# Sixteen instead of ten pairs of up-projection strips computed with seven block products for eight

## The chip, the core and the metric

The kernel runs on one core of a Trainium2 chip. The metric is the device time of one execution in microseconds (us), as the median of several runs. The engines are named as in the profile: PE is the tensor engine's matmuls, PEld its weight loads, DVE the vector engine, ACT the scalar engine, POOL and SP the two engines that here only issue DMAs.

## What is computed

A decoder trunk of two layers over 256 tokens with a width of 2048, in float32. The part that the change touches is the ConvFFN of each layer:

```python
def conv_ffn(h, w_up, conv_w, conv_b, w_down):
    u = causal_depthwise_conv(h @ w_up, conv_w, conv_b)
    gate, val = u[..., :D_FF], u[..., D_FF:]
    return (jax.nn.silu(gate) * val) @ w_down
```

`h` is 256 x 2048 and `w_up` is 2048 x 11264 (two halves of 5632 columns: gates and values). The convolution runs over three tokens, column by column. Attention, the other projections and the per-layer embedding stand before and behind it and stay as they are.

## The kernel before, in words

**Strips and blocks.** Every projection is cut into strips of 512 weight columns. A strip has 16 blocks of 128 weight rows. Loads bring four blocks at a time: `raw`, 128 x 4 x 512 numbers, 1 MB, from a pool of four buffers (`NRAW`). SP issues the loads in program order, and each waits until the buffer that it gets is read out. Two blocks make a tile (a word used below for this unit of work). ACT rounds a tile into `whi` (L305), DVE takes the rest, `wlo = raw - whi` (L306); both have four buffers (`NWSP`). This is called the split of a tile. PE then forms for each block and each of the two token halves three products (L342 to L344): `xl*whi`, `xh*wlo`, `xh*whi`, so that a tile takes 12 matmuls.

**Pairs and halves.** A gate strip `s` and the value strip `v = s + 11` that belongs to it follow each other; there are 11 such pairs in a layer. A layer does them in two parts: pairs 0 to 4, then the down projection of these, then pairs 5 to 10, then the rest of the down projection. Behind each up strip come the scaling out of PSUM (L540, ACT), the transposition through DRAM (L243 on DVE, L246 and L254 on POOL's queue), and, one strip later, the convolution (L905 on ACT, L908 to L914 on DVE), SiLU and product (L926, L927, L150, L151).

**Seven products for eight.** For a pair handled by the class `Seven`, the first four weight blocks of both strips and the first four blocks of `h` are taken as a 2 x 2 by 2 x 2 product of larger blocks, and multiplied with seven block products in place of eight, by a Winograd scheme. A block product is 6 matmuls (L455). The sums of tokens that it needs are made once for a layer (`block_sums`, L410 to L422). The weight sums are made on DVE in the raw buffers (`add`, L439), each of the seven weight operands is split like a tile (`parts`, L445 and L446), and DVE and ACT join the partial results in PSUM (L478, L485, L495 to L498). The four accumulators `c11`, `c21` (gates) and `c12`, `c22` (values) then go on through the other 12 blocks.

**Where the seven products stand.** `begin` hangs two loads (`load`) and the first four products into the value strip of the pair before: as hooks ahead of tiles 1, 3, 5 and 7 of its eight (`HEADS8`), the load ahead of tile 0. `go_on` hangs products five, six and seven into the pair's own gate strip, ahead of its tiles 0, 1 and 3 of six (`TAILS`). Since a pair begins inside the pair before it, and `after` is made only for every second pair, the pairs with seven products are 2 and 4 of the first part and 6, 8 and 10 of the second: ten in two layers. `HEADS6` is never used.

**What sets the order.** All is recorded by one program. A scheduler places instructions on each engine by priority; splits, adds and the joins in PSUM carry `tc.high_priority(offset=AHEAD)`, so they stand ahead of the convolution. Each engine works in its order, and a semaphore holds an instruction until what it reads is there and what it overwrites is free.

**Names used below.** G is the gate strip of a seven-product pair, V the value strip behind it. Counted from zero, G's tiles are G0 to G5 and V's V0 to V5, with the products between them. `c11` lies in the bank with the tag att, `c21` in one of five banks with the tag acc, `c12` and `c22` in the double bank `two`.

## Time and profile before

| | us |
|---|---|
| runs (3): lowest, median, highest | 2289.43, 2289.99, 2290.62 |
| profiled execution: its time | 2287.39 |
| profiled execution: its span in the trace | 2285.6 |
| PE busy | 2273.2 (99%) |
| DVE busy | 1620.8 (71%) |
| ACT busy | 1298.6 (57%) |

The span runs from the first to the last instruction; 1.8 us lie around it. The granted clock of the tensor engine is 0.999 over the span. In the groups of the profile, "busy" is the union of an engine's instructions, and a matmul's end is modelled, so that the spacing of starts tells more than the length of one. The seven products (L455) run between 446.0 and 2014.9 us.

### The profile page before, as it was taken

The page shows a single profiled execution, that of the slowest core. Times are in us where ns is not written, and L with a number is a line of the kernel's source. Part 1 is how long each engine was busy: PE and PEld are TensorE (multiplying, and loading weights), DVE is VectorE, ACT ScalarE, POOL GpSimd, SP SyncE. Part 2 cuts the span into 40 slices and gives each one's busy share as a digit, 9 for nine tenths or more (in the row PEclk, how much of TensorE's full clock was granted, in tenths as well). Part 3 has the DMA queues.
Part 4 walks back from the last instruction along what each step waited for, and adds up shares of the span by engine and source line. Part 5 has one row for each costly group of instructions (what it writes and reads, how often), then busy time and mean ns, then how long its engine had stood idle before and what let it go on. Part 6 is the DMA issues. An engine that isn't in the chain of part 4 may idle for free.

```text
span 2285.6 us, 27930 instructions
## 1 busy us (share of the span) xinstructions
PE 2273.2 (99%) x10137; PEld 1882.0 (82%) x10137; DVE 1620.8 (71%) x2335; ACT 1298.6 (57%) x1734; POOL 327.7 (14%) x575
## 2 busy tenths in 40 slices
PE   9999999999999999999999999999999999999998
PEld 7888888888888888888888888888888888888887
DVE  7666667788755888865667665768875588886565
ACT  6554555666634666644565554566663466664454
POOL 0311111111100111101111331211110011110100
PEclk9999999999999999999999999999999999999999
DMA  8777767676755767767676776768675577776763
GB/s 304 258 239 243 231 228 257 220 266 234 246 196 190 267 227 243 268 205 246 207 265 236 252 263 223 260 215 273 234 255 188 196 254 234 242 264 215 239 223 120
DMA packets 98346, 538.43 MB, mean 236 GB/s; under 512 B 16672, under 2 KB 17568, under 8 KB 46752
## 3 DMA queue, kind: packets, MB, share of 16 engines
q1 hardware_dynamic: 63360, 435.46, 54.6%
q0 software_dynamic: 32560, 95.98, 13.9%
q10 hardware_dynamic: 2288, 5.21, 0.6%
q8 instruction: 79, 1.29, 0.2%
q14 instruction: 59, 0.48, 0.1%
HBM read 486.52 MB, written 50.07 MB: 235 GB/s over the span
## 4 chain that ended last, share of the span: by engine, by line
PE 99%; DMA 0%; ACT 0%; DVE 0%; issue 0%; POOL 0%; SPq 0%; ACTq 0%
PE accv L343 26%; PE accv L342 26%; PE accv L344 26%; PE two L343 3%; PE two L342 3%; PE two L344 3%; PE gates L342 2%; PE gates L343 2%; PE gates L455 2%; PE gates L344 2%; PE two L455 2%; PE two L554 1%; PE keys L554 0%; DMA raw<-in_wqkv 0%; DMA turned<-there 0%; ACT whi L305 0%
## 5 line engine op out<-in xcount | busy, mean ns | idle before, releaser
L306 DVE TENSOR_TENSOR wlo<-raw,whi 128x1024 fp32r<-128x1024 f32 (+1 forms) x784 | 951.1, 1215 | 547.5 <-ACT whi L305 545.8
L305 ACT ACTIVATE whi<-raw 128x1024 fp32r<-128x1024 f32 (+1 forms) x784 | 825.7, 1054 | 776.1 <-PE accv L344 609.9
L342 PE MATMUL accv<-whi,h 128*128 128x512 f32 (+1 forms) x1688 | 655.3, 388 | 1.0 <-DVE h L144 0.9
L344 PE MATMUL accv<-whi,h 128*128 128x512 f32 (+1 forms) x1688 | 656.3, 389 | 0.0
L343 PE MATMUL accv<-wlo,h 128*128 128x512 f32 (+1 forms) x1688 | 655.9, 389 | 0.3 <-DVE wlo L306 0.2
L342 PEld LDWEIGHTS accv<-whi,h 128*128 128x128 f32 x1688 | 316.8, 188 | 67.4 <-ACT whi L305 1.6
L343 PEld LDWEIGHTS accv<-wlo,h 128*128 128x128 f32 x1688 | 316.9, 188 | 66.8 <-DVE wlo L306 2.0
L344 PEld LDWEIGHTS accv<-whi,h 128*128 128x128 f32 x1688 | 316.9, 188 | 64.9
L246 POOL DMA_DIRECT2D there<-y x162 | 91.4, 565 | 1275.4 <-DVE y L243 1257.1
L342 PE MATMUL accv<-whi,g 128*128 128x512 f32 x704 | 273.9, 389 | 0.0
L343 PE MATMUL accv<-wlo,g 128*128 128x512 f32 x704 | 273.9, 389 | 0.0
L344 PE MATMUL accv<-whi,g 128*128 128x512 f32 x704 | 273.9, 389 | 0.0
L254 POOL DMA_DIRECT2D turned<-there x324 | 189.6, 592 | 448.9 <-DMA there<-y 174.3
L343 PEld LDWEIGHTS accv<-wlo,g 128*128 128x128 f32 x704 | 132.1, 188 | 27.5
L342 PEld LDWEIGHTS accv<-whi,g 128*128 128x128 f32 x704 | 132.1, 188 | 27.4
L344 PEld LDWEIGHTS accv<-whi,g 128*128 128x128 f32 x704 | 132.1, 188 | 27.4
L446 DVE TENSOR_TENSOR wlo<-raw,whi 128x1024 fp32r<-128x1024 f32 x70 | 85.4, 1221 | 27.8 <-ACT whi L445 27.8
L445 ACT ACTIVATE whi<-raw 128x1024 fp32r<-128x1024 f32 x70 | 74.0, 1057 | 53.0 <-PE accv L344 47.6
L342 PE MATMUL gates<-whi,h 128*128 128x512 f32 x240 | 93.4, 389 | 0.0
L344 PE MATMUL gates<-whi,h 128*128 128x512 f32 x240 | 93.4, 389 | 0.0
L343 PE MATMUL gates<-wlo,h 128*128 128x512 f32 x240 | 93.4, 389 | 0.0
L342 PE MATMUL two<-whi,h 128*128 128x512 f32 x240 | 93.4, 389 | 0.0
(206 smaller groups left out, 2427.4 us busy)
## 6 DMA issues: line engine op xcount, KB each, us to landing
raw<-in_wup SPq DMA_DIRECT2D x176, 1024.0 KB, 5.5
raw<-in_wdn SPq DMA_DIRECT2D x88, 1024.0 KB, 5.0
there<-y POOLq DMA_DIRECT2D x171, 256.0 KB, 5.1
turned<-there POOLq DMA_DIRECT2D x324, 128.0 KB, 4.6
raw<-in_wqkv SPq DMA_DIRECT2D x40, 1024.0 KB, 5.7
raw<-in_wpg SPq DMA_DIRECT2D x32, 1024.0 KB, 4.8
raw<-in_wkv SPq DMA_DIRECT2D x24, 1024.0 KB, 5.6
raw<-in_wo_a SPq DMA_DIRECT2D x16, 1024.0 KB, 5.3
```

Source lines behind the costliest of these rows:

```text
L246: nc.gpsimd.dma_start(there[t * P : (t + 1) * P], y)
L254: nc.gpsimd.dma_start(z[32 * b : 32 * b + 32].rearrange("p a o r -> p a (o r)"), back[b])
L305: last["high"] = nc.scalar.activation(hi[:, c], r, AF.Copy).ins
L306: last["low weights"] = nc.vector.tensor_tensor(lo[:, c], r, f32(hi[:, c]), op=OP.subtract).ins
L342: nc.tensor.matmul(ps, xl, hi, start=first, stop=False, skip_group_check=again)
L343: nc.tensor.matmul(ps, xh, lo, start=False, stop=False, skip_group_check=again)
L344: nc.tensor.matmul(ps, xh, hi, start=False, stop=final, skip_group_check=again)
L445: last["high"] = nc.scalar.activation(hi, r, AF.Copy).ins
L446: last["low weights"] = nc.vector.tensor_tensor(lo, r, f32(hi), op=OP.subtract).ins
L455: nc.tensor.matmul(ps, x, y, start=begins, stop=ends, skip_group_check=True)
L554: run.append(nc.tensor.matmul(*args, skip_group_check=True, **kw).ins)
```

## The change

Every pair but the first two of the first part and the first of the second now gets seven: 2, 3 and 4, and 6 to 10, sixteen in two layers. Pairs then overlap: the four first products of the next pair stand in V of the one before, ahead of tiles 1, 2, 4 and 5 of its six (`HEADS[6]`), with the two loads ahead of tile 0. So that two pairs have room in PSUM, every second pair takes `c12` and `c22` from the five acc banks (`two=False`), and each accumulator is now allocated at the product that first writes it. `block_sums` makes the same sums with smaller operations and in other buffers (`room()`). `strip_among`, `go_on` and `end` are rewritten for this; `both` is defined and not called.

```diff
-HEADS8, HEADS6, TAILS = (1, 3, 5, 7), (1, 2, 4, 5), (0, 1, 3)
+HEADS, TAILS = {8: (1, 3, 5, 7), 6: (1, 2, 4, 5)}, (0, 1, 3)
...
-        f = four("whole").rearrange("p (k c) -> p k c", k=4)
-        for k in range(4):
-            nc.vector.tensor_tensor(f[:, k], f32(xs[k][:, :S]), f32(xs[k][:, S:]), op=OP.add)
...
+        out = [[] for _ in range(4)]
+        for i in range(2):
+            f, m = (room().rearrange("p (a c) -> p a c", c=P) for _ in range(2))
...
+        def value_bank(self, o):
+            if not self.two:
+                return bank("values", "acc")
+            if o == 0:
+                self.banks = two_banks()
+            return self.banks[:, o]
...
         def first(self):
-            self.c11, self.c21 = bank("gates"), bank("gates", "acc")
-            values = two_banks()
-            self.c12, self.c22 = values[:, 0], values[:, 1]
+            self.c11 = bank("gates")
...
         def second(self):
+            self.c12 = self.value_bank(0)
...
         def third(self):
+            self.c21 = bank("gates", "acc")
...
         def fourth(self):
+            self.c22 = self.value_bank(1)
...
         def begin(self, tiles):
-            do = [self.first, self.second, self.third, self.fourth]
-            self.hooks = {0: self.load, **dict(zip({8: HEADS8, 6: HEADS6}[tiles], do))}
-            return self.hooks
+            return {0: self.load, **dict(zip(HEADS[tiles], (self.first, self.second, self.third, self.fourth)))}
 
         def go_on(self):
-            return dict(zip(TAILS, (self.fifth, self.sixth, self.seventh)))
...
+            hooks = dict(zip(TAILS, (self.fifth, self.sixth, self.seventh)))
+            yield strip_among(self.W, self.strips[0], self.xs, hooks, [self.c11, self.c21], 4, self.base)
+
+        def end(self, hooks):
+            return strip_among(self.W, self.strips[1], self.xs, hooks, [self.c12, self.c22], 4, self.base)
...
+    def hooked(it, hooks):
+
+        for i in range(KB * 8):
+            if i in hooks:
+                hooks[i]()
+            try:
+                tile = next(it)
+            except StopIteration:
+                return
+            yield tile
...
                     v = s + FB // 4
-                    after = Seven(W, s + 1, v + 1, xs, sums) if j % 2 == (late is not None) and s + 1 in strips else None
+                    sums_next = (j > 0 or late is None) and s + 1 in strips
+                    after = Seven(W, s + 1, v + 1, xs, sums, two=j % 2 == 0) if sums_next else None
                     if j == 0 and late is not None:
                         yield from products([(W, s, 0), (W, v, 0)], xs, late, None)
-                        continue
-                    base = 4 if now else 0
-                    tiles = (len(xs) - base) // 2
-                    yield strip_among(W, s, xs, now.go_on() if now else {}, now and [now.c11, now.c21], base)
-                    yield strip_among(W, v, xs, after.begin(tiles) if after else {}, now and [now.c12, now.c22], base)
+                    elif now is None:
+                        yield strip_among(W, s, xs, {})
+                        yield strip_among(W, v, xs, after.begin(8) if after else {})
+                    else:
+                        yield from now.go_on()
+                        yield now.end(after.begin(6) if after else {})
                     now = after
```

On SP's queue, in the first layer's second part, this stood before from the last load of pair 6's gate strip on (`raw_1121`: tiles G4 and G5; the next three loads are the value strip's, the fifth is of the plain pair behind):

```order
L288 DMA raw_1121_6115<-in_wup 128x2048
L288 DMA raw_1139_6197<-in_wup 128x2048
L288 DMA raw_1144_6231<-in_wup 128x2048
L288 DMA raw_1149_6265<-in_wup 128x2048
L288 DMA raw_1165_6337<-in_wup 128x2048
```

And this stands there now (`raw_1131`: tiles G4 and G5; L471 are the two loads of `load` for pair 7; `raw_1151` holds V0 and V1, `raw_1163` V2 and V3):

```order
L288 DMA raw_1131_6139<-in_wup 128x2048
L471 DMA raw_1149_6221<-in_wup 128x2048
L471 DMA raw_1150_6223<-in_wup 128x2048
L288 DMA raw_1151_6225<-in_wup 128x2048
L288 DMA raw_1163_6287<-in_wup 128x2048
```

The first load of the value strip was second in this row and is now fourth. In the built program the fourth load of the row takes the buffer that the split of G3 frees, before and now; the second takes that of G1's split.

On DVE, before, from the split of G5 of the same pair on (`wlo_1141` is the split of V0, L243 the transposition of the gate strip's result, L908 the convolution):

```order
L306 TENSOR_TENSOR wlo_1125_6134<-raw_1121_6115,whi_1124_6133 128x1024
L914 TENSOR_TENSOR gate_1101_5992<-gate_1101_5992,over_1102_6005 128x7x4
L306 TENSOR_TENSOR wlo_1141_6200<-raw_1139_6197,whi_1140_6199 128x1024
L914 TENSOR_TENSOR gate_1101_5992<-gate_1101_5992,over_1103_6008 128x7x4x2
L306 TENSOR_TENSOR wlo_1143_6216<-raw_1139_6197,whi_1142_6215 128x1024
L306 TENSOR_TENSOR wlo_1146_6234<-raw_1144_6231,whi_1145_6233 128x1024
L243 STREAM_TRANSPOSE y_1129_6154<-u_1126_6149 128x4x4x32
L306 TENSOR_TENSOR wlo_1148_6250<-raw_1144_6231,whi_1147_6249 128x1024
```

And now, from the split of G5 on (`wlo_1153` is the split of V0, L456 are the splits for the products of pair 7 and L449 its weight sums):

```order
L306 TENSOR_TENSOR wlo_1135_6158<-raw_1131_6139,whi_1134_6157 128x1024
L934 TENSOR_TENSOR gate_1111_6016<-gate_1111_6016,over_1112_6029 128x7x4
L934 TENSOR_TENSOR gate_1111_6016<-gate_1111_6016,over_1113_6032 128x7x4x2
L306 TENSOR_TENSOR wlo_1153_6228<-raw_1151_6225,whi_1152_6227 128x1024
L456 TENSOR_TENSOR wlo_1157_6246<-raw_1149_6221,whi_1156_6245 128x1024
L449 TENSOR_TENSOR raw_1149_6221<-raw_1149_6221,raw_1150_6223 128x1024
L306 TENSOR_TENSOR wlo_1159_6259<-raw_1151_6225,whi_1158_6258 128x1024
L449 TENSOR_TENSOR raw_1150_6223<-raw_1150_6223 128x1024
L456 TENSOR_TENSOR wlo_1162_6276<-raw_1149_6221,whi_1161_6275 128x1024
L243 STREAM_TRANSPOSE y_1139_6178<-u_1136_6173 128x4x4x32
L449 TENSOR_TENSOR raw_1149_6221<-raw_1149_6221,raw_1150_6223 128x1024
L306 TENSOR_TENSOR wlo_1165_6290<-raw_1163_6287,whi_1164_6289 128x1024
```

Behind the split of V0, DVE's queue now holds two more splits and three weight sums up to the split of V2 (the last row), where before the split of V2 was the second behind it.

More of the change, by code (lines that the diff above doesn't have):

```diff
@@ L404, in block_sums @@
     def block_sums(xs):
-        f = four("whole").rearrange("p (k c) -> p k c", k=4)
-        for k in range(4):
-            nc.vector.tensor_tensor(f[:, k], f32(xs[k][:, :S]), f32(xs[k][:, S:]), op=OP.add)
-        (a11, a21), (a12, a22) = ((f[:, k : k + 2, :P], f[:, k : k + 2, P:]) for k in (0, 2))
-        m = four("sums").rearrange("p (q i c) -> p q i c", q=4, i=2)
-        nc.vector.tensor_tensor(m[:, 0], a21, a22, op=OP.subtract)
-        nc.vector.tensor_tensor(m[:, 1], a11, a21, op=OP.subtract)
@@ L415, in block_sums @@
-        nc.vector.tensor_tensor(m[:, 2], m[:, 0], a11, op=OP.subtract)
-        nc.vector.tensor_tensor(m[:, 3], m[:, 2], a12, op=OP.add)
-        out = []
-        for q in (0, 2):
+        out = [[] for _ in range(4)]
+        for i in range(2):
+            f, m = (room().rearrange("p (a c) -> p a c", c=P) for _ in range(2))
+            for a, k in enumerate((i, 2 + i)):
+                whole = f[:, 2 * a : 2 * a + 2].rearrange("p t c -> p (t c)")
+                nc.vector.tensor_tensor(whole, f32(xs[k][:, :S]), f32(xs[k][:, S:]), op=OP.add)
+            a11, a21, a12, a22 = (f[:, a] for a in range(4))
+            nc.vector.tensor_tensor(m[:, 0], a21, a22, op=OP.subtract)
+            nc.vector.tensor_tensor(m[:, 1], a11, a21, op=OP.subtract)
+            nc.vector.tensor_tensor(m[:, 2], m[:, 0], a11, op=OP.subtract)
+            nc.vector.tensor_tensor(m[:, 3], m[:, 2], a12, op=OP.add)
@@ L419, in block_sums @@
             hi, lo = (rt("sum", dt=F32R) for _ in range(2))
-            src = m[:, q : q + 2].rearrange("p q i c -> p (q i c)")
+            src = m.rearrange("p q c -> p (q c)")
             nc.scalar.activation(hi, src, AF.Copy)
             nc.vector.tensor_tensor(lo, src, f32(hi), op=OP.subtract)
-            for j in range(2):
-                out.append([[t[:, (2 * j + i) * P : (2 * j + i + 1) * P] for t in (hi, lo)] for i in range(2)])
+            for q in range(4):
+                out[q].append([t[:, q * P : (q + 1) * P] for t in (hi, lo)])
@@ L425, in block_sums, with __init__, token @@
         return out
     class Seven:
-        def __init__(self, W, s0, s1, xs, sums):
-            self.strips = W, s0, s1
-            self.sums = sums
-            self.token = lambda k, t: [[xs[k + i][:, c + t * P : c + (t + 1) * P] for c in (0, S)] for i in range(2)]
+        def __init__(self, W, s0, s1, xs, sums, base=0, two=True):
+            self.W, self.strips, self.base, self.two = W, (s0, s1), base, two
+            self.xs, self.sums = xs, sums
+        def token(self, k, t):
+            return [[self.xs[k + i][:, c + t * P : c + (t + 1) * P] for c in (0, S)] for i in range(2)]
@@ L457, in load @@
         def load(self):
-            W, s0, s1 = self.strips
             raws = []
-            for s in (s0, s1):
+            for s in self.strips:
                 raw = wraw.tile([P, RAW, 512], F32, tag="raw", name=nm("raw"))
-                nc.sync.dma_start(raw, W[s, 0])
+                nc.sync.dma_start(raw, self.W[s, self.base // RAW])
                 raws.append(raw)
@@ L509, in begin, with both, strip_among @@
         def begin(self, tiles):
[L510 to L512 removed]
+            return {0: self.load, **dict(zip(HEADS[tiles], (self.first, self.second, self.third, self.fourth)))}
         def go_on(self):
[L515 to L532 removed]
+            hooks = dict(zip(TAILS, (self.fifth, self.sixth, self.seventh)))
+            yield strip_among(self.W, self.strips[0], self.xs, hooks, [self.c11, self.c21], 4, self.base)
+        def end(self, hooks):
+            return strip_among(self.W, self.strips[1], self.xs, hooks, [self.c12, self.c22], 4, self.base)
+        def both(self):
+            yield from self.go_on()
+            yield self.end({})
+    def hooked(it, hooks):
[7 more added lines that the diff above has]
+            yield tile
+    def strip_among(W, s, xs, hooks, begun=None, skip=0, base=0):
+        n = len(xs) - skip
+        ps = begun or [bank("accv", "acc") for _ in range(2)]
+        it = hooked(weights(W, s, n, base=base + skip), hooks)
+        for k, o, hi, lo in (g for group in steps(it, n, 2) for g in group):
+            add_block(ps[o], xs[skip + k], o, hi, lo, k == 0 and not begun, k == n - 1, begun is not None)
         return ps
```

10 lines of the change are left out of this document (removed).

## Prediction

> **What bounds the kernel now.** First the page's head and the busy shares:
>
> ```profile
> span 2285.6 us, 27930 instructions
> ...
> PE 2273.2 (99%) x10137; PEld 1882.0 (82%) x10137; DVE 1620.8 (71%) x2335; ACT 1298.6 (57%) x1734; POOL 327.7 (14%) x575
> ```
>
> PE has work nearly all the time. Whether it also waits is in the view of the waits, for PE alone:
>
> ```profile
> PE warm L125 <- DVE zero L122: 1.2, 1, 1.2
> PE accv L342 <- DVE h L144: 0.9, 2, 0.7
> PE accv L343 <- DVE wlo L306: 0.2, 1, 0.2
> ```
>
> That is all: 2.3 us in the whole span. So time is saved by taking matmuls out, provided that nothing else becomes late. What a matmul costs is the spacing of starts. The timeline of PE gives it between the first product of a gate strip G and the first matmul of its value strip V, 90 matmuls later (12 for each of six tiles, 18 in products):
>
> ```profile
> 836.31 0.39 PE L455 MATMUL gates<-whi,h 128*128 128x512 f32 x1
> ...
> 856.71 0.39 PE L342 MATMUL two<-whi,h 128*128 128x512 f32 x1
> 856.94 0.39 PE L343 MATMUL two<-wlo,h 128*128 128x512 f32 x1
> ```
>
> 20.40 us by 90 is 0.2267 us each; the 0.39 us in the row overlap. Next, how full the other engines are, in windows of exactly one seven-product pair and one plain pair (7 x 6 + 24 x 6 and 32 x 6 matmuls, 378 in all, 85.68 us):
>
> ```profile
> 807.98:893.66 85.68, 85.68 (x379) 70.95 (x378) 72.49 (x110) 54.68 (x72) 13.89 (x24) 1.00 0.73 246
> 893.66:979.34 85.68, 85.68 (x379) 70.95 (x378) 71.29 (x110) 54.84 (x72) 13.89 (x24) 1.00 0.73 247
> ```
>
> In the order PE, PEld, DVE, ACT, POOL: DVE is busy for 72.5 and 71.3 us of 85.68, ACT for 55. The reader should keep DVE's 84% in mind, because the change turns the plain pair, where DVE rests, into another full one.
>
> **What is removed.** Six pairs lose one block product: 6 x 6 = 36 matmuls (the order of PE shows exactly 36 fewer). 36 x 0.2267 = 8.2 us. The bytes loaded stay the same, two loads of 1 MB standing for the first load of each strip.
>
> **What is added on DVE.** A seven-product pair has three splits more than a plain one, four weight sums and four joins in PSUM. Their spacing on DVE:
>
> ```profile
> 450.11 1.22 DVE L439 TENSOR_TENSOR raw<-raw,raw 128x1024 f32<-128x1024 f32 x1
> 451.25 2.35 DVE L306 TENSOR_TENSOR wlo<-raw,whi 128x1024 fp32r<-128x1024 f32 x2
> ...
> 836.40 0.69 DVE L496 TENSOR_TENSOR gates<-gates,part 128x512 f32<-128x512 f32 x1
> 837.00 0.70 DVE L243 STREAM_TRANSPOSE y<-u 128x512 f32<-128x512 f32 x1
> 837.63 0.67 DVE L497 TENSOR_TENSOR two<-part,gates 128x512 f32<-128x512 f32 x1
> ...
> 844.33 1.61 DVE L908 SCALAR_TENSOR_TENSOR gate<-turned,vec,gate 128x240 f32<-128x240 f32 x4
> ...
> 847.76 0.32 DVE L912 TENSOR_TENSOR over<-turned,vec 128x28 f32<-128x28 f32 x2
> ```
>
> A sum takes 1.14 us from start to start, a split 1.13 (2.35 less one length of 1.22), a join 0.60, a transposition 0.63, a convolution step 0.38 (1.61 less 0.46, by three); the four small ones of a strip (L912, L914) 0.12 each. So 7 x 1.14 + 4 x 0.60 = 10.4 us more than in a plain pair. Both together are 71.9 us (mean of the two windows), a seven-product pair is (71.9 + 10.4) / 2 = 41.1 us of DVE. Where pairs overlap PE needs 7 x 6 + 24 x 6 = 186 matmuls for one, 42.15 us. DVE has 1.0 us left in each: 98% full, but not over. That DVE can hold such a share is seen in the trace, in a stretch in which PE never stopped:
>
> ```profile
> 440.00:480.00 40.00, 40.00 (x179) 33.10 (x178) 38.05 (x52) 27.91 (x37) 4.60 (x8) 1.00 0.59 203
> ```
>
> ACT gets three roundings more and two copies, about 4 us; (54.8 + 4) / 2 is 29 us of 42.15: covered.
>
> A rule of the Trainium skill speaks against this (VectorE: DVE Perf Modes, section "The DRAIN you can't avoid"): the next vector operation does not start before the pipeline of the last is empty. By it each of some 60 operations of a pair would cost its full length, about 0.08 us more than the spacing above, and DVE would be the bound. The rows just shown contradict it: 837.00 is before 836.40 + 0.69. I keep it as a rival with a small chance.
>
> **What is moved: the load of the value strip.** While a pair's sums stay in two of the four raw buffers, the other loads share the rest. In the new order the loads that follow G's last one on SP are two for the next pair, and only then the first of V, which waits for the split of G3 and so is fourth in a burst. Before, the load in that place belonged to the last tiles of V and had time. Its row, three times, with the start of G ahead of it, and what SP's issue and landing were (last number of the DMA row: us to landing):
>
> ```profile
> 750.63 0.39 PE L455 MATMUL gates<-whi,h 128*128 128x512 f32 x1
> 758.76 0.33 SPq L288 DMA_DIRECT2D raw<-in_wup  x1
> raw<-in_wup SPq DMA_DIRECT2D x1, 1024.0 KB, 9.4
> 844.43 0.33 SPq L288 DMA_DIRECT2D raw<-in_wup  x1
> raw<-in_wup SPq DMA_DIRECT2D x1, 1024.0 KB, 11.6
> 2009.72 0.39 PE L455 MATMUL gates<-whi,h 128*128 128x512 f32 x1
> 2017.83 0.33 SPq L288 DMA_DIRECT2D raw<-in_wup  x1
> raw<-in_wup SPq DMA_DIRECT2D x1, 1024.0 KB, 12.3
> ```
>
> It is issued 8.1 us after G starts and lands at 17.5, 19.7 and 20.4 us. From landing to a split tile takes the rounding and the subtraction:
>
> ```profile
> 852.20 1.04 ACT L305 ACTIVATE whi<-raw 128x1024 fp32r<-128x1024 f32 x1
> 853.28 1.23 DVE L306 TENSOR_TENSOR wlo<-raw,whi 128x1024 fp32r<-128x1024 f32 x1 [2.08 <-ACT whi L305]
> ```
>
> 852.20 to 854.51, 2.3 us, 2.4 with the semaphore. PE reaches V at 20.4 us and reads `wlo` with its second matmul, at 20.6. So V0 is late by 17.5 + 2.4 - 20.6 (not late), by 1.5 and by 2.2 us, 1.2 in the mean. In the kernel before V0's load was second in the burst. The wait is ACT's, and queued behind it on ACT are the roundings for the next pair's first product and for V1 and the scaling of `c11`; on DVE all behind the split of V0 waits with it. This comes to pass in the first seven-product pair of each part, 4 times: 4.9 us. These places are well founded, since up to V0 nothing differs from the trace.
>
> **And the later pairs, where DVE has no rest before.** There are 8 more such places (3 in the first part, 7, 8 and 9 in the second, in two layers). Where V0 is late DVE has stood idle, and it then has the rest of V and of G in one queue. From the split of V0 to that of G3 of the next pair it has all of a pair but the part from G3 to V0: three splits, eight convolution steps, a transposition and four small ones, 3 x 1.14 + 8 x 0.38 + 0.63 + 0.5 = 7.6 us. That leaves 41.1 - 7.6 = 33.5 us. Then G3's buffer is free, V's load is issued, lands after L us, and 2.4 us later V0 is split: a loop of 35.9 + L against PE's 42.15. PE stalls from L = 6.25 us on. For L in such a place the trace has a load alone, and one that is third in a burst:
>
> ```profile
> raw<-in_wup SPq DMA_DIRECT2D x1, 1024.0 KB, 5.0
> raw<-in_wup SPq DMA_DIRECT2D x1, 1024.0 KB, 6.6
> ```
>
> (issued at 830.44 and 843.30). The ends are 5.0 (nothing lost) and 12.3 (6.1 us lost each). What drew the fourth load out is the traffic on POOL's queue at that time, as the windows in its flight and before it show (last two numbers: DMA share, GB/s), with POOL's four `turned` transfers:
>
> ```profile
> 850.00:857.00 7.00, 7.00 (x33) 5.79 (x32) 4.09 (x5) 3.79 (x5) 0.00 (x0) 1.00 1.03 229
> 842.00:844.00 2.00, 2.00 (x10) 1.67 (x9) 2.00 (x3) 1.02 (x2) 0.56 (x1) 1.00 1.00 416
> ...
> 846.06 2.34 POOL L254 DMA_DIRECT2D turned<-there x4 [3.45 <-ACT whi L305]
> ```
>
> The 16 engines are full in both, but carry half the bytes once `turned` is on them. In a later pair the gate strip's transpositions stand behind the splits of G2 and beside G3, so `turned` comes some 5 us behind the load, not 2, and I place L near the third in a burst: 7.1 us. The loop is 43.0, 0.85 us lost in each, 8 x 0.85 = 6.8 us.
>
> The page "DMA: Bandwidth & Descriptors" of the Trainium skill (section "Anatomy of one DMA") has 2.0 us and the bytes at 436 GB/s for a DMA; 1 MB would land in an estimated 4.4 us, V0 would never be late and the sum would be the 8.2 us alone. The lone load above took 5.0, and none in a burst was near 4.4.
>
> **Inside V.** Behind V0's split stand, up to V2's, seven operations of 1.14 us and a transposition, 8.6 us; PE is there after 36 matmuls, 8.2 us. 0.4 us late; the loop holds this already, except behind the last late V of each part: 4 x 0.4 = 1.6 us.
>
> **Edits at nothing.** `block_sums` has 14 operations on DVE for 10, some half as long, about 0.3 us a layer while the down projection ahead has DVE at rest. The bank of `c11` must be scaled out before the next pair's first product: `c11` ends six matmuls before G does, and V0 gives 2.7 us more; the scaling is one row of ACT:
>
> ```profile
> 855.55 0.69 ACT L540 ACTIVATE u<-gates,rcol 128x512 f32<-128x512 f32 x1 [0.25 <-PE gates L344]
> ```
>
> 1.4 + 2.7 - 0.7 leaves 3.4 us; with V0's load late, three roundings stand ahead of it on ACT, and about 1 us is left. If that goes too, PE waits for ACT at the first product. The acc banks come round after five uses, a strip and more.
>
> **Sum.** -8.2 + 4.9 + 6.8 + 1.6 = +5.1 us. The profiled execution took 2287.4 us (span 2285.6 and 1.8 around it) and would take 2292.5; the median of the runs is 2.6 us above it, so 2295.1 us. About 0.2%, 4.6 us, is what a measurement of this kernel can tell.
>
> **Rivals.**
>
> Nothing is late (faster). The lead of four split buffers and a quick load hide all, and the matmuls alone count: 2290.0 - 8.2 = 2281.8 us. For it: PE waits nowhere today, the stretch at 440 us with DVE at 95%, loads alone at 5.0 us. Against it: two of the three landings above. 0.20.
>
> Only the first places are late: L is under 6.25 in the later pairs, 4.9 + 1.6 us remain, 2288.3 us. For it: the new spacing of the loads on DVE's queue. Against it: DVE's 1.0 us of rest. 0.15.
>
> The load is drawn out everywhere (slower by more). If `turned` meets V's load in the later pairs as it does at 844 us, L is 9.4 or above, and the loop 45.3: 3.15 us x 8 = 25 us, with the 6.5 us of the first places 2290.0 + 23.5 = 2313.5 us. It decides from L = 9 on. For it: three rows. Against it: the later `turned`. 0.11.
>
> DVE is the bound: each operation costs its length, 60 x 0.08 us added to 41.1 gives 45.9 us a pair, 3.7 over PE in 12 overlapping strips, 45 us: 2326 us. Against it the rows above. 0.04. That is the rule on the drain.
>
> That the change doesn't do what it says is excluded by the order of PE.
>
> **How the numbers follow.** My forecast has 0.50 and its own range is 2290 to 2301: L from 6.6 to 7.6 and the first places from 0.5 to 1.9 us each. Of it 0.20 lies within 0.2%, 0.30 above. The rival of the first places gives 0.13 to no change and 0.02 to faster. So faster 0.20 + 0.02 = 0.22, same 0.20 + 0.13 = 0.33, slower 0.30 + 0.11 + 0.04 = 0.45. The range goes from just under the first rival, 2281, to 2304; what is left out is most of the two slow rivals and some tail, under 0.2.
>
> **What the new profile would show.** PE's waits, now 2.3 us, would name `whi` or `wlo` and add up to some 13 us; they would lie at the first tile of V, about 12 places, with ACT's rounding of it ended by the DMA `raw<-in_wup`. The issue of that load would be 8.1 us after G in the first pairs, later (about 11) in the following ones. DVE's busy time per overlapping pair would be near 41 us. I am wrong if PE's waits stay under 3 us (nothing is late), if they lie at other tiles or on PSUM banks (the wrong wait), or if the load lands within 6 us in a burst.

## The result, and the profile after

| | before | changed |
|---|---|---|
| runs, of one chip | 4 | 4 |
| lowest, median, highest | 2289.15, 2289.71, 2290.62 | 2304.74, 2310.62, 2313.31 |
| profiled execution, its span | 2287.39, 2285.6 | 2304.74, 2303.0 |
| ratio of the times | | 1.0087, 95% interval 1.0070 to 1.0103 |

The change makes the kernel slower by 0.9%, where 0.2% was forecast. The sign is as forecast, the size is outside the range (2281 to 2304). The profiled execution is the fastest of the four; what is read from it explains 17.4 us of span, and the median lies 6 us above it. The spread of the runs has grown from 1.5 to 8.6 us.

The head of the page and its busy shares:

```profile
span 2303.0 us, 27972 instructions
...
PE 2273.0 (99%) x10101; PEld 1875.6 (81%) x10101; DVE 1676.3 (73%) x2409; ACT 1312.1 (57%) x1764; POOL 327.7 (14%) x575
```

The 36 matmuls are gone (10101 for 10137), and DVE has 55 us more (six pairs by 10.4 us were forecast to be 62). PE's "99%" is the same only by rounding: outside its busy time lie 30.0 us of the span now and 12.4 us before. And PE is as busy as before with 8.2 us of matmuls fewer, since the modelled end of a matmul that waits covers a part of the wait. The view of PE's waits:

```profile
PE gates L342 <- DVE values L507: 9.2, 6, 1.8
PE gates L342 <- DVE two L507: 4.3, 6, 1.5
PE two L343 <- DVE wlo L306: 2.3, 6, 0.8
PE values L343 <- DVE wlo L306: 1.3, 2, 1.1
```

The last two lines are waits at the splits of V, but V0 itself, where the prediction placed them, is late in two pairs only (the first of each second part, by 0.9 and 1.7 us); the others stand at later tiles of V, mostly V2. The first two are new: 12 waits, one in the G behind each overlap, at the second token half of G0, the first matmul that goes on with `c21`, and they end with L507 on DVE. By the spacing of starts over 0.2267 us (the matmul after a wait is late by another 0.11) the waits in V cost some 7 us and those at `c21` 16.8 us.

Here is one of them, first PE (its row names the releaser), then DVE in the same 4 us:

```profile
885.04 0.39 PE L342 MATMUL gates<-whi,h 128*128 128x512 f32 x1
...
886.17 0.39 PE L344 MATMUL gates<-whi,h 128*128 128x512 f32 x1
888.02 0.50 PE L342 MATMUL gates<-whi,h 128*128 128x512 f32 x1 [1.46 <-DVE values L507]
```

```profile
884.24 0.69 DVE L505 TENSOR_TENSOR part<-values,part 128x512 f32<-128x512 f32 x1
884.94 1.22 DVE L456 TENSOR_TENSOR wlo<-raw,whi 128x1024 fp32r<-128x1024 f32 x1
886.08 0.69 DVE L506 TENSOR_TENSOR gates<-gates,part 128x512 f32<-128x512 f32 x1
886.68 0.69 DVE L508 TENSOR_TENSOR values<-values,part 128x512 f32<-128x512 f32 x1
887.28 0.69 DVE L507 TENSOR_TENSOR values<-part,gates 128x512 f32<-128x512 f32 x1
```

L506 has put the sum into `c21` at 886.77, and PE still waits until 887.97. The reason is in the operands: L507 is `c22 = q - c21`. It reads `c21`, so PE may not write it until L507 is done. In the kernel before, the same join ended at 838.30 (its row is in the prediction), and PE came to `c21` 12 matmuls after 836.31, at 839.03. The slack was 0.73 us, and it stood in rows that the prediction quotes.

The load that the prediction speaks of, in the pair before that wait, from the timeline: G, the load's issue, ACT's rounding that waited for it, the split of V0, and the same load's issue one pair later:

```profile
840.56 0.39 PE L465 MATMUL gates<-whi,h 128*128 128x512 f32 x1
...
850.81 0.33 SPq L288 DMA_DIRECT2D raw<-in_wup  x1
...
858.86 1.06 ACT L305 ACTIVATE whi<-raw 128x1024 fp32r<-128x1024 f32 x1 [5.20 <-DMA raw<-in_wup]
...
859.95 1.23 DVE L306 TENSOR_TENSOR wlo<-raw,whi 128x1024 fp32r<-128x1024 f32 x1 [2.63 <-ACT whi L305]
...
894.46 0.33 SPq L288 DMA_DIRECT2D raw<-in_wup  x1
```

The view of the DMAs has its time from issue to landing, the last number:

```profile
raw<-in_wup SPq DMA_DIRECT2D x1, 1024.0 KB, 7.9
```

Landing at 18.2 us after G; DVE stands idle for 2.6 us; the split ends at 861.18, and 33.3 us of DVE's queue later (33.5 was forecast) the next such load is issued. All parts of the loop are there. But V0 itself is in time, at 861.9. What is late is the join at the end of the next stretch: from 861.18 DVE needs 26.8 us to the end of L507 (26.1 to 27.5 in the twelve pairs), and PE for the same stretch only 24.5 (108 matmuls, V and 12 of G). So V0 has to be split 2.3 us before PE comes to it, and its load has to land 15.7 us after G (20.4 + 24.5 - 26.8 - 2.4), not 18.2 as the prediction had it.

That gives an account with no number fitted: from behind the wait at `c21` in its own G ("own loss") to the end of that in the next G, a pair loses the landing after G, less 15.7, less the own loss. The 15.7 is from the one pair above; landings are from SP's rows, losses from the starts on PE:

| G at | landing | own loss | account | measured |
|---|---|---|---|---|
| 471.47 (first) | 16.5 | 0 | 0.8 | 0.7 |
| 513.63 | 17.8 | 0.7 | 1.4 | 1.5 |
| 752.61 (first) | 19.1 | 0 | 3.4 | 3.5 |
| 796.33 | 18.8 | 2.0 | 1.1 | 0.9 |
| 840.56 | 18.2 | 0.9 | 1.6 | 1.7 |
| 883.68 | 18.9 | 1.7 | 1.5 | 2.3 |
| 1566.11 (first) | 16.6 | 0 | 0.9 | 0.9 |
| 1608.26 | 18.0 | 0.9 | 1.5 | 1.6 |
| 1847.43 (first) | 19.9 | 0 | 4.2 | 4.3 |
| 1891.93 | 20.1 | 2.0 | 2.4 | 2.2 |
| 1936.73 | 20.0 | 1.7 | 2.6 | 2.5 |
| 1981.41 | 19.4 | 2.0 | 1.7 | 1.1 |
| sum | | | 23.1 | 23.2 |

Row by row the two differ by up to 0.8 us.

The span follows. The four stretches with products, each from its first product to the last matmul of its last value strip, take 774.6 us together and took 758.2: -8.2 for the matmuls and +24.6 for PE's waits (the table's 23.2, the rest in V of the last pairs and in small delays of single matmuls). With +1.0 at the start (PE is 1.0 us later at 125 us, before the change begins) that is +17.4, as measured.

### The profile page after: what moved, and what is told of

It reads as the page before. It is cut to its first block, busy times and chain, and to the rows that moved or that the text cites. A ratio compares the mean times of both kernels' runs of the same rounds, so it can differ in the third digit from the quotient of the medians.

```text
span 2303.0 us, 27972 instructions
## 1 busy us (share of the span) xinstructions
PE 2273.0 (99%) x10101; PEld 1875.6 (81%) x10101; DVE 1676.3 (73%) x2409; ACT 1312.1 (57%) x1764; POOL 327.7 (14%) x575
## 3 DMA queue, kind: packets, MB, share of 16 engines
q10 hardware_dynamic: 2288, 5.21, 0.6%
## 4 chain that ended last, share of the span: by engine, by line
PE 75%; DVE 15%; DMA 5%; issue 3%; ACT 1%; POOL 0%; DVEq 0%; ACTq 0%; POOLq 0%
PE accv L343 22%; PE accv L342 22%; PE accv L344 22%; DVE wlo L306 5%; DMA raw<-in_wup 4%; DVE wlo L456 4%; DVE raw L449 2%; DVE val L928 2%; PE two L574 1%; PE gates L342 1%; PE gates L343 1%; PE gates L344 1%; PE two L343 1%; PE two L344 1%; PE two L342 1%
## 5 line engine op out<-in xcount | busy, mean ns | idle before, releaser
L306 DVE TENSOR_TENSOR wlo<-raw,whi 128x1024 fp32r<-128x1024 f32 (+1 forms) x760 | 920.7, 1214 | 507.3 <-ACT whi L305 506.3
L342 PE MATMUL accv<-whi,h 128*128 128x512 f32 (+1 forms) x1304 | 507.0, 389 | 1.2 <-DVE h L144 1.2
L344 PE MATMUL accv<-whi,h 128*128 128x512 f32 (+1 forms) x1304 | 507.9, 389 | 0.0
L343 PE MATMUL accv<-wlo,h 128*128 128x512 f32 (+1 forms) x1304 | 507.2, 389 | 0.0
L342 PEld LDWEIGHTS accv<-whi,h 128*128 128x128 f32 x1304 | 245.2, 188 | 52.1 <-ACT whi L305 2.1
L344 PEld LDWEIGHTS accv<-whi,h 128*128 128x128 f32 x1304 | 245.4, 188 | 50.1
L343 PEld LDWEIGHTS accv<-wlo,h 128*128 128x128 f32 x1304 | 245.3, 188 | 50.2 <-DVE wlo L306 0.2
L342 PE MATMUL gates<-whi,h 128*128 128x512 f32 x384 | 150.9, 393 | 13.6 <-DVE values L507 9.2
L342 PEld LDWEIGHTS accv<-whi,g 128*128 128x128 f32 x704 | 132.2, 188 | 27.5
L456 DVE TENSOR_TENSOR wlo<-raw,whi 128x1024 fp32r<-128x1024 f32 x112 | 136.6, 1219 | 18.5 <-ACT whi L455 18.4
L343 PE MATMUL gates<-wlo,h 128*128 128x512 f32 x384 | 149.7, 390 | 0.0
L344 PE MATMUL gates<-whi,h 128*128 128x512 f32 x384 | 149.6, 390 | 0.0
L455 ACT ACTIVATE whi<-raw 128x1024 fp32r<-128x1024 f32 x112 | 118.2, 1055 | 49.8 <-PE accv L344 18.4
L342 PEld LDWEIGHTS gates<-whi,h 128*128 128x128 f32 x384 | 72.1, 188 | 33.3 <-DVE values L507 11.8
```

What stands on the lines that cost most here:

```text
L306: last["low weights"] = nc.vector.tensor_tensor(lo[:, c], r, f32(hi[:, c]), op=OP.subtract).ins
L342: nc.tensor.matmul(ps, xl, hi, start=first, stop=False, skip_group_check=again)
L343: nc.tensor.matmul(ps, xh, lo, start=False, stop=False, skip_group_check=again)
L344: nc.tensor.matmul(ps, xh, hi, start=False, stop=final, skip_group_check=again)
L455: last["high"] = nc.scalar.activation(hi, r, AF.Copy).ins
L456: last["low weights"] = nc.vector.tensor_tensor(lo, r, f32(hi), op=OP.subtract).ins
```

## The experiments

Three theories. **L+D**: a loop; V0's load is late, DVE idles for it, and DVE's queue, full to 96%, cannot make that up before the join at `c21`; both halves are needed, the load (L) and the full queue (D). **J**: the joins simply stand too far back in DVE's queue for G0, whatever the load does. **C**: the other edits (block sums, banks) cost something by themselves. From e4 on **D** alone is named as well: DVE's queue is too full, wherever the loads stand. Every time below is a median, with the ratio to the kernel before on the same chip (2288 to 2289 us there); differences between experiments are differences of medians, and by the ratios they come out up to 3 us otherwise.

**e1, ten pairs.** The condition of before, everything else of the change:

```diff
-                    sums_next = (j > 0 or late is None) and s + 1 in strips
-                    after = Seven(W, s + 1, v + 1, xs, sums, two=j % 2 == 0) if sums_next else None
+                    sums_next = j % 2 == (late is not None) and s + 1 in strips
+                    after = Seven(W, s + 1, v + 1, xs, sums) if sums_next else None
```

> The changed program with only the condition put back, so that ten pairs in two layers are made with seven products and none overlap; the new block sums, the hooks and the allocation of the accumulators stay. Theory A (all of the loss comes from pairs that overlap): the time of before, 2289.7 us, within 1.5. Theory C (the other edits cost something by themselves, block sums or banks): above 2292 us.

2288.35 us, ratio 0.9999 (0.9991 to 1.0008). C falls: block sums, hooks and allocations cost nothing. All of the loss comes from the overlap.

**e2, the pair's loads behind V0's.**

```diff
+            do = [self.first, self.second, self.third, self.fourth]
+            if tiles == 6:
+                do[0] = lambda: (self.load(), self.first())
-            return {0: self.load, **dict(zip(HEADS[tiles], (self.first, self.second, self.third, self.fourth)))}
+            return {**({0: self.load} if tiles == 8 else {}), **dict(zip(HEADS[tiles], do))}
```

> The changed kernel, where the two loads for the next pair are issued behind the first load of the value strip instead of ahead of it (only in strips of six tiles, so for the overlapping pairs). Theory L (the late load of V0 is the root: DVE stands idle for it, and the wait at c21 four strips of work later is its echo): V0 and c21 waits both go at the overlapping pairs, 24 us of stalls less some 3 at first pairs, so near 2288 us or below. Theory J (the joins stand too far back in DVE's queue for G0's second half, whatever the load): only the waits at V0 go, some 3 us, the 16.8 us at c21 stay, and the time is 2305 to 2310 us.

2293.16 us, ratio 1.0023 (1.0011 to 1.0034): 17 us less than the changed kernel, by the order of three DMAs alone. PE's waits in the trace:

```profile
PE gates L342 <- DVE two L507: 3.9, 4, 1.6
PE gates L342 <- DVE values L507: 3.1, 3, 1.4
```

The waits at V0 are gone, and of the 12 at `c21` seven are left. In the pair at 836.27 the load is issued 4.3 us after G and lands in 5.2 (7.9 in the changed kernel):

```profile
840.53 0.33 SPq L288 DMA_DIRECT2D raw<-in_wup  x1
```

```profile
raw<-in_wup SPq DMA_DIRECT2D x1, 1024.0 KB, 5.2
```

So the waits at `c21` were mostly the load's echo, as L says. J, which left them all, falls. But L's own number (2288 or below) is missed too: some 10 us of waits stay in this trace, by the spacing of starts.

**e3, the joins earlier.** `third` and `fourth` one tile earlier, and so the joins:

```diff
-HEADS, TAILS = {8: (1, 3, 5, 7), 6: (1, 2, 4, 5)}, (0, 1, 3)
+HEADS, TAILS = {8: (1, 3, 5, 7), 6: (1, 2, 3, 4)}, (0, 1, 3)
```

> The changed kernel with the four first products ahead of tiles 1, 2, 3 and 4 of a strip of six instead of 1, 2, 4 and 5: 12 more matmuls, 2.7 us, stand between the fourth product and the first use of c21, and some steps of the convolution go behind the joins on DVE. Theory J: the 12 waits at c21 (0.6 to 1.9 us, 16.8 in all) go; V0 is reached earlier and may wait up to 1 us more in each of 12 places; 2294 to 2304 us. Theory L: DVE is as late as before by the load, the waits turn up at V0, V1 or the next splits with the same sum, and the time is 2305 to 2311 us.

2308.79 us, ratio 1.0089 (1.0075 to 1.0103): nothing gained.

```profile
PE values L343 <- DVE wlo L306: 5.1, 9, 0.8
PE two L343 <- DVE wlo L306: 4.8, 10, 0.8
PE values L342 <- ACT whi L305: 2.7, 3, 1.3
```

Not one wait at `c21` is left, and the same time is lost at the splits. The join was the tightest place, not the cause: a late queue shows at whichever deadline comes first.

**e4, both.** The edits of e2 and e3 together.

> Both edits of the two kernels before it. Theory L: as the moved load alone, near 2288 us or below. Theory J: both kinds of wait go at the overlapping pairs, those of the first pairs (about 3 us) stay, so 2289.7 - 8.2 + 3 = 2284 to 2287 us. If DVE's 40 us of work for 42 us of PE is itself too much (theory D), waits remain somewhere and the time stays above 2292 us.

2290.90 us, ratio 1.0012 (1.0001 to 1.0023). By the medians 2 us better than e2, which the intervals do not separate. It lies between what the theories gave: not near 2284 (J), above 2288 (L) and under 2292 (D). "DVE too full" is now the open part.

**e5, less work on DVE, the load untouched.** It leaves out two of the three taps of the value strips:

```diff
-                for d in (1, 2):
+                for d in () if value else (1, 2):
                     c = runs[:, o, :, d:]
```

> The changed kernel; it leaves out the second and third tap of the convolution of the value strips, so 8 steps on DVE (L928, 0.38 us each, 3.05 us) fewer in each pair; loads and matmuls stay as they are. Theory L+D (a loop: from the split of V0 DVE has 33.3 us of work up to the split of G3 that frees the buffer, then the load lands 8.0 us later, then 2.4 us for the split, 43.7 us against PE's 42.15): the loop falls to 40.7, nothing is late in the later pairs, and at the first pairs V0 may land 18.7 us after G in place of 15.7, so 0 to 1.2 us are lost in each of four: 2281 to 2284 us. Theory L alone (the landing of the load sets it, whatever DVE has to do): no change from the changed kernel, 2305 to 2311 us.

2298.93 us, ratio 1.0045 (1.0031 to 1.0058): 12 us less than the changed kernel, so the load alone is not it; but far from 2284, so the arithmetic of the loop was wrong somewhere. The trace shows where. In the pair at 841.02:

```profile
841.02 0.39 PE L465 MATMUL gates<-whi,h 128*128 128x512 f32 x1
...
850.20 0.33 SPq L288 DMA_DIRECT2D raw<-in_wup  x1
...
861.13 1.06 ACT L305 ACTIVATE whi<-raw 128x1024 fp32r<-128x1024 f32 x1 [4.24 <-DMA raw<-in_wup]
```

```profile
raw<-in_wup SPq DMA_DIRECT2D x1, 1024.0 KB, 10.8
```

With DVE early the load is issued 9.2 us after G, and takes 10.8 instead of 7.9: it lands at 20.0 all the same. In the 12 pairs the landings are 16.7 to 20.7. What POOL issued while the load was in flight, in e5 and in the changed kernel:

```profile
851.70 2.34 POOL L254 DMA_DIRECT2D turned<-there  x4 [3.31 <-DMA there<-y]
```

```profile
849.97 0.57 POOL L246 DMA_DIRECT2D there<-y  x1 [10.06 <-DVE y L243]
851.70 0.56 POOL L246 DMA_DIRECT2D there<-y  x1 [1.15 <-DVE y L243]
```

A faster DVE made the request earlier, and there the load met the four `turned` transfers, as in the first pairs, in place of the two `there` writes. So it is in all eight later pairs of e5. The waits are all but one at V now (threshold 18.2 us; by it the 12 landings give 10.8 us at V0, measured 10.5).

**e6, one weight sum on POOL.**

```diff
-            self.add(self.u, self.b12, self.b22)
+            with tc.high_priority(offset=AHEAD):
+                nc.gpsimd.tensor_tensor(self.u, self.b12, self.b22, op=OP.add)
```

> The changed kernel with one of the four weight sums of each pair (b12 + b22, needed only by the third product) on POOL instead of DVE: 1.14 us less on DVE in each pair. Loop theory: 42.55 us against 42.15, so about half of the 25 us of waits goes: 2294 to 2300 us. Rival: the sum stands in POOL's queue ahead of the turning transfers and waits there for its load, or DVE and POOL hinder each other, and the time is 2305 us or more.

2336.28 us, ratio 1.0214 (1.0199 to 1.0230), the rival's side and worse. POOL's sum, and the split that DVE starts beside it:

```profile
827.42 3.15 POOL L483 TENSOR_TENSOR raw<-raw 128x1024 f32<-128x1024 f32 x1 [6.21 <-DVE raw L449]
```

```profile
828.24 0.70 DVE L243 STREAM_TRANSPOSE y<-u 128x512 f32<-128x512 f32 x1
828.87 2.80 DVE L456 TENSOR_TENSOR wlo<-raw,whi 128x1024 fp32r<-128x1024 f32 x1
```

The sum takes 3.15 us, and the split 2.80 in place of 1.22: it ends 1.1 us after POOL does. DVE loses more (1.6) than it is relieved of (1.14), in twelve pairs some 5 of the 26 us against the changed kernel. The trace has most of the rest: in the eight later pairs V0's load takes 10.0 us in the mean in place of 8.1, some 15 us in all: `turned` transfers fly beside each of these loads, and in the changed kernel beside one alone, for its last 0.2 us.

**e7, e6 with the loads behind V0's.**

> The kernel with the loads for the next pair behind V0's load (2293.2 us), and the sum b12 + b22 on POOL as well. If what is left there is DVE's 40 us in 42 (theory D), the 8 us of waits at c21 go: 2281 to 2285 us, faster than before. If POOL's queue hinders, 2290 us or more.

2302.34 us, ratio 1.0059 (1.0046 to 1.0071): 9 us worse than e2. In each of its 16 sums on POOL, too, the split beside it ends 1.1 us after the sum.

**e8, PE comes to c21 later.** e2, and in G the halves of G0 and G1 are ordered by token half, with the sixth product ahead of G2:

```diff
-HEADS, TAILS = {8: (1, 3, 5, 7), 6: (1, 2, 4, 5)}, (0, 1, 3)
+HEADS, TAILS = {8: (1, 3, 5, 7), 6: (1, 2, 4, 5)}, (0, 2, 3)
...
+            if k0 < head:
+                held.append((k0, hi, lo))
+                if k0 == head - 2:
+                    for o in range(outs):
+                        for g, hi, lo in held:
+                            yield [(g + i, o, hi[i], lo[i]) for i in range(2)]
+                    held = []
...
-            yield strip_among(self.W, self.strips[0], self.xs, hooks, [self.c11, self.c21], 4, self.base)
+            yield strip_among(self.W, self.strips[0], self.xs, hooks, [self.c11, self.c21], 4, self.base, head=4)
```

> The kernel with the loads for the next pair behind V0's load (2293.2 us), and in G the second token half of G0 behind the first half of G1 (the sixth product moves ahead of G2), so that PE comes to c21 six matmuls, 1.36 us, later. Theory J (only the place of the joins is left): waits of 0.5 to 1.8 us at c21 fall to 0 to 0.5, 2284 to 2287 us. Theory D (DVE is late by its whole queue): the waits turn up at the next splits with the same sum, 2290 to 2294 us.

2294.47 us, ratio 1.0024 (1.0013 to 1.0034), as e2. The waits at `c21` shrink to 0.3 us and less and turn up at the splits (up to 1.3), as theory D says. J is out here too.

**e9, half a megabyte less ahead of V0.** Order as in the change, but of the first of the two loads only `b11`'s half goes ahead:

```diff
+                c = slice(0, 2 if k == 0 else 4)
-                nc.sync.dma_start(raw, self.W[s, self.base // RAW])
+                nc.sync.dma_start(raw[:, c], self.W[s, self.base // RAW, :, c])
...
+        def load_rest(self):
+            with tc.issue_after(last["load"]):
+                nc.sync.dma_start(self.b21, self.W[self.strips[0], self.base // RAW, :, 2:4])
```

> The changed kernel, but the first load for the next pair is cut in two, and its second half (b21, needed from the fourth product on) is issued behind V0's load: 0.5 MB less ahead of V0. At the 379 GB/s that the engines carried in V0's flight that is 1.4 us. By the account of the trace (lost in a pair = landing of V0's load after G, less 15.7 us, less what its own G has lost already) the first pairs lose 0 to 2.8 us, 4.8 in four, and the loop of the later ones is 33.3 + 2.4 + 6.6 = 42.3, 0.15 us over PE: 6 to 9 us of waits in place of 25, and 2290 to 2296 us. If the place of V0's load among the others does not matter (theory J or D): 2305 to 2311 us.

2306.34 us, ratio 1.0067 (1.0052 to 1.0082). A miss. V0's load lands earlier only in three of the four first pairs (15.6, 17.8 and 17.5 us after G); in the later ones it takes 7.8 to 8.6 us, no less than in the changed kernel. There it is issued about 11 us after G in most pairs, when the load that was cut has landed already (at 10.2, in the pair at 793.84), and the half put behind it now flies beside it. The time is where J or D had it, but since the load did not land earlier, the run does not test them. What it shows is that half a megabyte moved from ahead of the load to beside it leaves its time as it was.

**e10, e11, e12, e15: towards a better order.** e10 is e2 with the first load in two halves (`b11`, second load, `b21`). e11 adds the join that reads `c21` always ahead of that of `c12`. e12 adds e3's `HEADS`. e15 also puts `b21`'s half behind the load of V2 and V3:

```diff
+            do[0] = (lambda: (self.load_rest(), self.first())) if tiles == 8 else (lambda: (self.load(), self.load_rest(), self.first()))
...
-                nc.vector.tensor_tensor(self.c22, self.q, self.c21, op=OP.subtract)
-                nc.vector.tensor_tensor(self.c12, self.c12, self.p, op=OP.subtract)
+                free = nc.vector.tensor_tensor(self.c22, self.q, self.c21, op=OP.subtract).ins
+                with tc.issue_after(free):
+                    nc.vector.tensor_tensor(self.c12, self.c12, self.p, op=OP.subtract)
...
+                do[2] = lambda: (self.load_rest(), self.third())
```

> Both loads for the next pair behind V0's load (2293.2 us), and of the first of them only the half with b11 ahead of the second load, so that b12 lands 1.4 us or more earlier. In the trace of the kernel with both behind, DVE stood idle for 1.5 us at the sum b11 + b12 for that load, and the waits at c21 came behind it. If that is what is left: 2284 to 2290 us. If DVE's 40 us in 42 are what is left (theory D), it stays at 2291 to 2294 us.

> As the kernel before, and the join that reads c21 (c22 = q - c21) is always ahead of the one of c12 on DVE, so that PE may write c21 one join, 0.6 us, earlier where the value accumulators are in the acc banks. If waits of up to 0.6 us at c21 are all that is left: 1 to 3 us faster than the kernel before. If DVE's queue is late as a whole, the same time.

> As the kernel before, and the first products ahead of tiles 1, 2, 3 and 4 of six. With the loads no longer late the earlier joins should count now: 2282 to 2287 us, which would be faster than the kernel before the change. If DVE is late as a whole (theory D), the waits move to the splits of V with the same sum, and it is no faster than its neighbour.

> The kernel with both loads behind V0's, in halves, joins in the better order and the first products ahead of tiles 1 to 4 (2289.8 us), and the half with b21 issued behind the load of V2 and V3 as well, which landed 24 to 26 us after G there and was late at V2 in some pairs. If the loads are what is left: 2283 to 2287 us, faster than the kernel before. If DVE's load of work is (theory D): 2288 to 2291 us.

2293.41 (ratio 1.0013, 1.0004 to 1.0023), 2293.82 (1.0016, 1.0006 to 1.0027), 2289.76 (0.9997, 0.9988 to 1.0007) and 2289.61 us (1.0009, 1.0000 to 1.0018). Of the gains hoped for only that of `HEADS` came, and not in full: e12 is 4 us faster than e11, where D had nothing and the other forecast 7 to 12. e12 and e15 stand level with the kernel before; none of the orders beats it.

**e13, more traffic beside the load.** The changed kernel with a second, unread copy of what is written back:

```diff
+            if twice:
+                spare = dram.tile([P, 512], F32, tag="spare", name=nm("spare"))
+                nc.gpsimd.dma_start(spare, y)
```

> The changed kernel, where each up strip's transposed halves are written to DRAM twice (a spare copy that nobody reads): 0.5 MB more per strip on POOL's queue, in the later pairs mostly while V0's load is in flight. Theory L+D (the loop 33.3 + 2.4 + L, with L drawn out by what is in flight beside it): at 379 GB/s 0.5 MB is 1.4 us, L goes from 8.0 to about 9.4 and each of 8 later pairs loses 1.4 us more, the first pairs up to 1: 11 to 16 us, 2320 to 2327 us. If L does not matter to the time (J or D alone): 2308 to 2313 us.

2322.39 us, ratio 1.0152 (1.0133 to 1.0171), as L+D had it. In the eight later pairs of its trace the load takes 8.8 to 10.8 us, 9.4 in the mean, for 8.1. One of them, issue and flight:

```profile
856.04 0.33 SPq L291 DMA_DIRECT2D raw<-in_wup  x1
```

```profile
raw<-in_wup SPq DMA_DIRECT2D x1, 1024.0 KB, 8.9
```

**e14, the loads early and less work on DVE.** The edits of e2 and e5 together.

> Both loads for the next pair behind V0's load (2293.2 us), and the second and third tap of the convolution of the value strips left out (8 steps on DVE, 3.05 us a pair). Theory D for what is left there (DVE's 40 us in 42 have no room for its waits): nothing is late and the 36 matmuls alone count, 2281 to 2284 us. If what is left comes from loads (b12, V2) or from the transfers that ACT waits for: 2288 to 2293 us.

2279.97 us, ratio 0.9961 (0.9946 to 0.9977), 8.0 us under the kernel before: the 36 matmuls, whole. It leaves out two taps of the value strips, so it is a test and no faster version of the kernel. Three waits of PE are left in the trace, none in the up strips:

```profile
PE accv L342 <- DVE h L144: 1.9, 1, 1.9
PE warm L125 <- DVE zero L122: 1.2, 1, 1.2
PE accv L343 <- DVE wlo L306: 0.7, 1, 0.7
```

In one pair of it DVE is busy for 38.1 of 42.2 us; in the changed kernel for 40.3 of 43.0 and 44.5, two pairs:

```profile
845.00:887.20 42.20, 42.20 (x188) 34.96 (x187) 38.14 (x53) 29.10 (x38) 6.74 (x12) 1.00 0.72 246
```

```profile
845.00:888.00 43.00, 41.56 (x184) 34.07 (x182) 40.26 (x61) 27.76 (x38) 6.94 (x12) 1.00 0.69 240
888.00:932.50 44.50, 42.79 (x187) 34.77 (x187) 40.34 (x60) 29.02 (x39) 6.96 (x12) 1.00 0.63 234
```

With the load early and DVE full (e2), small waits of DVE come through to PE. This is e2's DVE, with 3.6 us of idle time within 5 us:

```profile
854.26 1.22 DVE L456 TENSOR_TENSOR wlo<-raw,whi 128x1024 fp32r<-128x1024 f32 x1 [2.07 <-ACT whi L455]
856.98 1.23 DVE L449 TENSOR_TENSOR raw<-raw,raw 128x1024 f32<-128x1024 f32 x1 [1.49 <-DMA raw<-in_wup]
```

e14 has such waits as well, but 4 us of room for them in each pair. So both halves are shown: the load (e2 against the change, e14 against e5: 17 and 19 us) and DVE's room (e5 against the change, e14 against e2: 12 and 13 us). Not separated is whether the eight steps left out count by their time or by their place in the queue.

## Why the prediction was right and wrong, point by point

**The saving** was right: 36 matmuls, 8.2 us by count, 8.0 in e14, where nothing waits.

**DVE's 41.1 us** was right in size: 40.3 in each of two pairs. "98% full, but not over" was taken as cover, and here it is none: the stretch at 440 us with DVE at 95% showed only that PE can go on for 40 us beside a full DVE while nothing upstream of DVE is late. e14 against e2 prices the missing room at 13 us.

**The moved load** was right as the cause: e2. The landings at the first pairs (16.5 to 19.9) are near those read from the kernel before (17.5 to 20.4); the later issue (10.8 us after G in the mean, about 11 forecast), DVE's 33.5 us (33.3) and the 0.4 us at V2 (0.2 to 0.4, once 1.3) are as forecast.

**The step that failed first** is "V0 is late by 17.5 + 2.4 - 20.6": it took V0's split for the deadline of the load. The deadline is the join at `c21`, 2.5 us tighter: DVE needs 26.8 us from V0's split to L507 where PE needs 24.5 from the start of V, and 0.2 more come from `wlo` being read by V's second matmul. With the threshold at 15.7 instead of 18.2 the four first pairs lose 9.4 us (0.7, 3.5, 0.9 and 4.3 measured) and not 4.9. This is the case that the prediction named as "the wrong wait", and its numbers stood in the rows quoted: L497 and the start of G leave `c21` 0.73 us. What was costed for the joins was their length, not when they must be done. e3 adds that the join is only where it shows first: with it out of the way the lost time is the same, at the splits. What the step left out is the whole queue behind V0's split.

**The term mis-sized** is "L near the third in a burst: 7.1 us". It was 8.1 in the mean of eight. The prediction looked for `turned` and found it behind the load, rightly; it overlooked the two `there` writes beside it (POOL's rows under e5) and the second load for the next pair, which is issued 1.7 us ahead. In that flight the 16 engines are full:

```profile
850.80:858.80 8.00, 8.00 (x37) 6.62 (x36) 6.49 (x15) 1.20 (x2) 0.56 (x1) 1.00 0.98 379
```

One us more of L is one us more per pair: the loop is 33.3 + 2.4 + 8.1 = 43.8, 1.65 over PE's 42.15, not 0.85. The eight later pairs lose 13.8 us (the table's other rows), where the prediction had 6.8 and 1.6 at V2. e13 confirms the slope: with 1.3 us more of L the eight later pairs of its trace lose some 8 us more, where the loop gives 10.4. Together the two steps make 23.2 out of 13.3 us.

**"Edits at nothing"** was right: e1.

**Luck.** The sign was forecast by a small margin, 0.45 against 0.33 for no change. The wait that cost most, 16.8 us at `c21`, was in no term of the sum; that a slower kernel was forecast at all rests on waits at V0, of which two of the twelve came.

**The rivals.** "The load is drawn out everywhere" (2313.5, chance 0.11) came nearest in time, but by luck: L is 8.1 and not 9.4, `turned` did not meet the load in the later pairs, and the rest is the 2.5 us less room. "DVE is the bound" by the length of each operation is out: L508 starts at 886.68 and L507 at 887.28, before 886.68 + 0.69. The rule of the Trainium skill (VectorE: DVE Perf Modes, section "The DRAIN you can't avoid") that no next operation starts before the pipeline of the last is empty is not what these rows show; the same section adds that an operation that is not held starts earlier, which the prediction left out and which these rows allow. The 4.4 us for 1 MB that the prediction works out from the Trainium skill (DMA: Bandwidth & Descriptors, section "Anatomy of one DMA") rest on a fit that the section gives for DMAs issued from POOL, and these loads are SP's: alone they took 4.7 us or more, as V0's load in the later pairs 7.7 to 9.1. The sum did not use it.

**Left open**: why the other runs of the changed kernel are up to 8.6 us above the profiled one. That landings differ from pair to pair by up to 3.6 us within one execution fits, but no trace shows the other executions.

## What to carry to other kernels

An engine that is 96% busy, as DVE is here, gives little cover: lateness of its input goes on through its whole queue, and shows at the first deadline that is tighter than the input's own. So price a late load not at its first reader but at every place downstream where the waiting engine has less slack than there, and look for reads that hold a buffer (here a join that reads what the matmul will write). And look at what flies beside a load: in e5 an earlier request landed no earlier.

## What the runs showed of the hardware

**DVE and POOL.** In e6 a vector operation with two operands from SBUF, started while POOL added in SBUF, ended 1.1 us after POOL did (2.80 for 1.22 us), while a transposition with one operand ran at its usual 0.70 beside it. The 1.1 us recur at all 16 sums of e6 and all 16 of e7. POOL's sum itself took 3.2 to 3.3 us where such a split was running as it started, and 2.4 where none was. The Trainium skill (SBUF — State Buffer, section "SBUF: two separate sides") has it that the port pair the two share is locked for a whole instruction and that the other one waits. The rows agree with it.

**The clock after a wait.** In e10 PE waited 2.7 and 0.8 us with one matmul between, and 0.9 us after the second the granted clock fell to half for 3.4 us (it is the number ahead of the last two of a row: 0.50 for 1.00). The two waits, and the windows ahead of the fall and from it on:

```profile
912.28 0.50 PE L342 MATMUL values<-whi,h 128*128 128x512 f32 x1 [2.73 <-ACT whi L305]
913.55 0.50 PE L343 MATMUL values<-wlo,h 128*128 128x512 f32 x1 [0.76 <-DVE wlo L306]
```

```profile
911.00:914.41 3.41, 1.37 (x5) 0.92 (x6) 2.15 (x4) 3.41 (x6) 0.00 (x0) 1.00 0.00 0
914.41:917.82 3.41, 3.41 (x10) 2.63 (x9) 3.41 (x6) 2.12 (x3) 0.00 (x0) 0.50 0.36 96
```

The same came in e11 behind waits of 2.4 and 0.8 us, in e13 behind 1.3 and 0.8, each for 3.4 us, and in e15 behind one of 2.1 (with another of 0.8 after the fall), for 6.8 us. The starts were 0.43 us apart in these stretches, so that one of 3.4 us costs some 1.6 us (an estimate: eight matmuls by 0.2). No single wait at `c21`, up to 1.8 us, did it, and in the changed kernel the granted clock stays full through all the waits of the pairs. The Trainium skill (TensorE: Matmul & The Clock Gate, section "Part 1: The HAM clock gate (the "warmup" mystery)") puts the fall to half the clock behind an idle window of about 3.4 us. The length of the falls, 3.4 us or twice that, agrees with such a window; the idle time does not, since PE was idle for 2.0 us in all in e13, with a matmul between, and nowhere for 3.4 us in a row.
